# Layer boundaries: the residual's scale and shift on VectorE inside the next layer, parameter columns issued later, the second router's weights read earlier

## The chip, the cores and the metric

One core of a Trainium2 chip runs the whole program in one launch. The metric is the device time of one execution in microseconds (us). Of the kernel before there are three timed runs and one execution that was profiled.

## What is computed

The reference runs two blocks of two layers each on a sequence of 512 rows of 1024 values in float32. Each layer is a mixer, a residual sum with a layer norm, a feed-forward part, and again a residual sum with a layer norm. The mixers are RWKV, gated delta net (gdn), a state space mixer (ssd) and dilated attention; the feed-forward part is a gated linear unit (ffn) in the first block and a mixture of 32 experts with a router (MoE) in the second. The norm that stands at each of the eight boundaries is this:

```python
def _layer_norm(x, g, b):
    mu = jnp.mean(xf, -1, keepdims=True)
    var = jnp.mean(jnp.square(xf - mu), -1, keepdims=True)
    return ((xf - mu) * lax.rsqrt(var + LN_EPS) * g + b).astype(x.dtype)
...
x = _layer_norm(DEEPNORM_ALPHA * x + (1 + ga1) * y, ln_g[i, 0], ln_b[i, 0])
u = x * (1 + sc2) + sh2
```

The next layer needs the norm's output twice: at once, as the input of its matmuls, and much later, as the residual x of its own sum.

## The kernel before

The residual lies in four tiles `res[:, t]` of 128 rows by 1024 values. A layer's matmuls run with the input transposed. A float32 product is made of three matmuls of halves: `split` writes the high half of an operand with ScalarE (`uh`, `wh`, line L370) and the low half with VectorE (`ul`, `wl`, line L371). `Stream` loads the weights by SyncE (SP) into three buffers `raw` and splits them into a ring of five `wh`/`wl` slots (the pool `wsp`), some tiles ahead of TensorE.

A layer ends with `ln_tail` (L488). For each tile t it makes the last sum, the norm's statistics, and then `Norm.norm`: the mean and variance, `rs` with a power on POOL (L376), `mr` on VectorE (L2391), and the normalisation in place on ScalarE (L2396, or L2394). `Norm.trans` transposes the tile on TensorE and applies the norm's g and b, folded with the layer's own scale and shift, per partition (L615), so that the matmuls do not need `res` with g and b in it. The first matmul blocks of the next layer, the "heads" (L406), are issued here in two halves of 256 columns; the second half waits for the last tile. Then `Norm.finish` puts g and b on the residual itself, four multiplications and four additions of 128x1024 on POOL, with rows that SP loaded:

```python
with self.n.tc.issue_after(self.last):
    for t in range(NT):
        G.tensor_mul(res[:, t], res[:, t], self.g)
        G.tensor_add(res[:, t], res[:, t], self.b)
```

This runs at five boundaries, l = 0 to 3 (into the first ffn, gdn, the second ffn, ssd) and l = 5 (into attention); the last norm, l = 7, has a form of its own. Ahead of a MoE (l = 4 and 6, `keep=True`) the MoE applies it itself. A scheduler sets the order of each engine's instructions when the program is built, and it does not change at run time; each engine works through its own list in order.

Each mixer also reads small parameters and brings them into columns: for gdn the convolution's weights and the norm's gains (`gconv`, `gng`), the casts `negb` and `idb`; for ssd `sconv`, `snw`, `hv` and `dsk` (L1423, element by element, L1424 halves it). `moe_open` (L1898) reads the router's weights `rw`, `rb` and `gs` through ScalarE's DMA queue (L1914 to L1917); at the first router its calls stand well ahead of the norm, at the second right behind attention.

## Time and profile before

| what | value |
|---|---|
| median of 3 runs | 3842.15 us (3834.15 to 3850.82) |
| the profiled execution | 3842.46 us |
| its span in the trace | 3840.6 us |
| mean granted TensorE clock | 0.957 |
| TensorE busy | 3561.0 us, 93% |
| VectorE (DVE) busy | 1904.9 us, 50% |
| ScalarE (ACT) busy | 1153.1 us, 30% |
| POOL busy | 554.3 us, 14% |

The span is what the trace holds of the profiled execution; 1.9 us lie around it. In time order the stages are RWKV up to about 630 us, the first ffn (from 660), gdn (1040), the second ffn (1560), ssd (1936), the first MoE (2355), attention (2885) and the second MoE (3254).. The granted clock is 1.00 at 2.4 GHz and 0.50 at 1.2 GHz.

### The profile page before, as it was taken

To read this page: it belongs to the slowest core of one execution; us is meant where nothing else is said; L and a number is where in the kernel's file an instruction comes from. 1 tells how busy PE (TensorE), PEld (TensorE's weight loads), DVE (VectorE), ACT (ScalarE), POOL (GpSimd) and SP (SyncE) were. 2 spreads that over 40 slices of the span, in tenths; PEclk is the share of its full clock that TensorE was granted. 3 is DMA by queue.
4 is the path that set the end of the run, shared out by engine and by line. 5 is a ranking of instruction groups with operands and counts; after the bars stand their busy time and mean duration, and the time that the engine had idled before them with its cause. 6 is when DMAs were issued, how large, how long until landed. Compare 5 with 4: busy or idle time off the path is not lost. (4 is left out here: it accounts for less than half of the span.)

```text
span 3840.6 us, 53459 instructions
## 1 busy us (share of the span) xinstructions
PE 3561.0 (93%) x21818; PEld 2441.1 (64%) x21818; DVE 1904.9 (50%) x3405; ACT 1153.1 (30%) x2216; POOL 554.3 (14%) x326
## 2 busy tenths in 40 slices
PE   7999998999989998999979998999997998899998
PEld 5666656788766655788868777454446776545444
DVE  6766657433676555534469875222225344322223
ACT  4544433322343333422244432111113333211111
POOL 0111114301321120312121110200003111200001
PEclk9999998999999988999989998999998998899999
DMA  6323444223221111232323453999992224598997
GB/s 234 122 83 121 136 154 140 99 88 109 76 67 50 45 36 65 88 99 88 96 82 114 144 182 118 392 419 375 419 381 80 63 64 151 222 413 345 371 419 300
DMA packets 273357, 676.90 MB, mean 176 GB/s; under 512 B 27565, under 2 KB 166662, under 8 KB 224982
## 3 DMA queue, kind: packets, MB, share of 16 engines
q1 hardware_dynamic: 264998, 669.35, 47.1%
q10 hardware_dynamic: 7824, 3.06, 0.3%
q8 instruction: 173, 2.83, 0.3%
q0 software_dynamic: 288, 1.05, 0.1%
q14 instruction: 74, 0.61, 0.0%
HBM read 660.92 MB, written 12.48 MB: 175 GB/s over the span
## 5 line engine op out<-in xcount | busy, mean ns | idle before, releaser
L371 DVE TENSOR_TENSOR wl<-raw,wh 128x1024 fp32r<-128x1024 f32 x305 | 412.1, 1352 | 430.2 <-ACT wh L370 424.3
L384 PE MATMUL acc<-uh,wh 128*128 128x512 f32 x1384 | 559.1, 406 | 2.5 <-ACT uh L370 2.5
L370 ACT ACTIVATE wh<-raw 128x1024 fp32r<-128x1024 f32 x305 | 320.3, 1052 | 795.4 <-PE acc L384 383.5
L384 PE MATMUL acc<-uh,wl 128*128 128x512 f32 x1384 | 542.0, 392 | 0.0
L384 PE MATMUL acc<-ul,wh 128*128 128x512 f32 x1384 | 541.8, 392 | 0.0
L2046 PE MATMUL acc<-raw,xg 128*64 128x512 f32 x2048 | 448.6, 593 | 3.8 <-DMA raw<-in_moe_w_up_dram 3.8
L2046 PEld LDWEIGHTS acc<-raw,xg 128*64 128x64 f32 x2048 | 149.8, 137 | 293.3 <-issue 273.9
L384 PEld LDWEIGHTS acc<-uh,wh 128*128 128x128 f32 x1384 | 261.3, 189 | 65.5 <-issue 11.3
L384 PEld LDWEIGHTS acc<-ul,wh 128*128 128x128 f32 x1384 | 261.3, 189 | 57.2 <-issue 6.4
L384 PEld LDWEIGHTS acc<-uh,wl 128*128 128x128 f32 x1384 | 260.8, 188 | 56.3 <-issue 0.8
L257 POOL TENSOR_TENSOR raw<-raw,gar 128x1024 f32<-128x1024 f32 x60 | 155.4, 2608 | 588.5 <-DMA raw<-in_ffn_w_out_dram 341.8
L2046 PE MATMUL acc<-raw,hT 128*64 128x512 f32 x1024 | 233.7, 601 | 3.5 <-issue 1.9
L2167 DVE TENSOR_TENSOR h<-h,acc 128x512 f32<-128x512 f32 x32 | 22.0, 688 | 395.8 <-PE acc L2046 395.8
L376 POOL TENSOR_TENSOR rs<-rs,mhalf 128x1 f32<-128x1 f32 x32 | 18.9, 591 | 1184.9 <-DVE rs L375 728.6
L2046 PEld LDWEIGHTS acc<-raw,hT 128*64 128x64 f32 x1024 | 72.0, 138 | 140.5 <-issue 136.2
L2158 DVE SCALAR_TENSOR_TENSOR mrow<-acc,sg,mrow 128x512 fp32r<-128x512 f32 x64 | 47.9, 750 | 199.9 <-ACT mrow L2157 196.7
L434 PE MATMUL o<-wh,hl 128*128 128x512 f32 x352 | 138.6, 394 | 0.0
L434 PE MATMUL o<-wh,hh 128*128 128x512 f32 x352 | 138.3, 393 | 0.0
L434 PE MATMUL o<-wl,hh 128*128 128x512 f32 x352 | 136.7, 388 | 0.0
L384 PE MATMUL tp<-uh,wh 128*128 128x512 f32 x312 | 136.4, 437 | 0.0
L2046 PE MATMUL tp<-mrow,ul 128*128 128x256 f32 x512 | 130.6, 294 | 4.0 <-DVE mrow L2051 4.0
L384 PE MATMUL tp<-ul,wh 128*128 128x512 f32 x312 | 132.7, 425 | 0.0
(661 smaller groups left out, 6351.6 us busy)
## 6 DMA issues: line engine op xcount, KB each, us to landing
raw<-in_moe_w_up_dram SPq DMA_DIRECT2D x128, 1024.0 KB
raw<-in_moe_w_gate_dram SPq DMA_DIRECT2D x126, 1024.0 KB
raw<-in_moe_w_down_dram SPq DMA_DIRECT2D x74, 1024.0 KB
raw<-in_moe_w_down_dram SPq DMA_DIRECT2D x108, 512.0 KB
raw<-in_ada_w_dram SPq DMA_DIRECT2D x48, 1024.0 KB
raw<-in_ffn_w_in_dram SPq DMA_DIRECT2D x44, 1024.0 KB
raw<-in_ffn_w_out_dram SPq DMA_DIRECT2D x20, 1024.0 KB
raw<-in_attn_w_qkv_dram SPq DMA_DIRECT2D x36, 512.0 KB
```

The lines of the kernel that those rows point to most:

```text
L257: n.nc.gpsimd.tensor_mul(src, src, row[:, None, :].to_broadcast(list(src.shape)))
L370: self.nc.scalar.activation(dst_h, src, AF.Copy)
L371: self.nc.vector.tensor_sub(dst_l, src, dst_h.bitcast(F32))
L376: self.pow_ins = self.nc.gpsimd.tensor_tensor(out, out, self.mhalf[:, :out.shape[1]], op=ALU.pow).ins
L384: self.nc.tensor.matmul(ps, lhsT=l[:, k], rhs=r[:, k], start=n == 0, stop=n == 3 * NK - 1)
L434: self.nc.tensor.matmul(ps, lhsT=l[:, kx0 + k, ts], rhs=r[:, k], start=start and n == 0, stop=stop and n == 5)
L2046: self.tc.keep_in_program_order(PE.matmul(*a, **k))
L2158: V.scalar_tensor_tensor(yl[:, cs], y[half], g, yh[:, cs].bitcast(F32), op0=ALU.mult, op1=ALU.subtract)
L2167: V.tensor_tensor(to(h), to(h), of(pu), op=ALU.mult)
```

## The change

Four things change.

- At l = 0, 1, 2 and 5 the g and b of the residual are no longer applied by POOL in `finish`. The new `affine` does it on VectorE inside the next layer: in an ffn behind the third block of the first group, in gdn and in attention behind the first projection group. The row of g is loaded by SP behind the newest weight load, the row of b by POOL's queue. In an ffn the two rows have a pool of their own, in gdn and attention they take slots of the ring `wl`. At l = 3 (into ssd) POOL does it as before.
- In gdn and ssd the parameter columns, casts and exponentials are issued behind the last head matmul, split and activation (`after`).
- In ssd the two element-wise DMAs of `dsk` go from SP's queue to POOL's, and the halving of `dsk` comes later (L1482).
- The second router's weights and gains are read in `moe_small`, ahead of attention, into a pool of their own.

The diff:

```diff
@@ -347,7 +347,7 @@
-    def load_rows(self, name, parts, pool=None, q=None, rt=None):
+    def load_rows(self, name, parts, pool=None, q=None, rt=None, late=False):
@@ -361,14 +361,24 @@
         ps = self.tp(name=name + "_p")
-        nc.tensor.transpose(ps[:, :n], rt[:n, :], self.ident[:n, :n])
         out = (pool or self.const).tile([P, n], F32, name=name)
-        nc.vector.tensor_copy(out, ps[:, :n])
+        with self.after(late):
+            nc.tensor.transpose(ps[:, :n], rt[:n, :], self.ident[:n, :n])
+            nc.vector.tensor_copy(out, ps[:, :n])
         yield out
+    @contextmanager
+    def after(self, late=True):
+        with ExitStack() as es:
+            if late:
+                for i in (self.last_mm, self.last_split, self.last_act):
+                    es.enter_context(self.tc.issue_after(i))
+            yield
...
         self.nc.scalar.activation(dst_h, src, AF.Copy)
-        self.nc.vector.tensor_sub(dst_l, src, dst_h.bitcast(F32))
+        self.last_split = self.nc.vector.tensor_sub(dst_l, src, dst_h.bitcast(F32)).ins
@@ -403,8 +413,9 @@
             for l, r in ((w[0], self.uh), (w[0], self.ul), (w[1], self.uh)):
-                self.nc.tensor.matmul(ps[:, cs], lhsT=l[:, k], rhs=r[:, k, cs], start=n == 0, stop=n == 3 * NK - 1)
+                mm = self.nc.tensor.matmul(ps[:, cs], lhsT=l[:, k], rhs=r[:, k, cs], start=n == 0, stop=n == 3 * NK - 1)
                 n += 1
+        return mm.ins
@@ -506,7 +517,7 @@
         for ps, w in heads:
-            self.mm_t_half(ps, w, 1)
+            self.last_mm = self.mm_t_half(ps, w, 1)
         self.pre = [h[0] for h in heads]
@@ -574,6 +585,20 @@
+    def affine(self, tile):
+        nc, V = self.nc, self.nc.vector
+        for n, (q, f) in enumerate(((nc.sync, V.tensor_mul), (nc.gpsimd, V.tensor_add))):
+            row = tile()
+            if n:
+                q.dma_start(row, bcast_rows(self.late[n]))
+            else:
+                with self.tc.issue_after(self.st.loads[max(self.st.loads)]):
+                    q.dma_start(row, bcast_rows(self.late[n]))
+            for t in range(NT):
+                f(self.res[:, t], self.res[:, t], row)
@@ -637,7 +662,7 @@
             ln = Norm(self, pool, l)
-            hp, ep = pool("ffh"), pool("ffe", 2)
+            hp, ep, ap = pool("ffh"), pool("ffe", 2), pool("ffa", 2)
             self.load_gate(i, 1)
@@ -650,6 +675,8 @@
                     self.split(hh[:, b], hl[:, b], sg)
+                    if g is FF_GROUPS[0] and b == 2:
+                        self.affine(lambda: ap.tile([P, D], F32, name="row"))
                 last = g is FF_GROUPS[-1]
@@ -1144,16 +1171,17 @@
             negb = cn.tile([P, C], BF, name="negb")
-            V.tensor_copy(negb, self.hcv("gneg"))
             idb = cn.tile([P, P], BF, name="idb")
-            V.tensor_copy(idb, self.ident)
-            cw = self.rows_to_cols("gconv", [I["gdn_conv"][0]], pool=cn).rearrange("p (i b) -> p i b", i=4)
-            ng = self.rows_to_cols("gng", [I["gdn_norm_g"][0]], pool=cn)
-            V.tensor_scalar(ng, ng, 0.5, None, op0=ALU.mult)
             dtb = cn.tile([P, 2, H], F32, name="dtb")
...
             nc.sync.dma_start(dtb[:, 1], bcast_rows(I["gdn_a_log"][0]))
-            A.activation(dtb[:, 1], dtb[:, 1], AF.Exp)
+            cw = self.rows_to_cols("gconv", [I["gdn_conv"][0]], pool=cn, late=True).rearrange("p (i b) -> p i b", i=4)
+            ng = self.rows_to_cols("gng", [I["gdn_norm_g"][0]], pool=cn, late=True)
+            with self.after():
+                V.tensor_copy(negb, self.hcv("gneg"))
+                V.tensor_copy(idb, self.ident)
+                V.tensor_scalar(ng, ng, 0.5, None, op0=ALU.mult)
+                A.activation(dtb[:, 1], dtb[:, 1], AF.Exp)
             Q = cn.tile([P, 8, 2, C], F32, name="gQ")
@@ -1374,6 +1402,7 @@
             drain(proj(0))
+            self.affine(lambda: self.wsp.tile([P, D], F32, name="row", tag="wl"))
             for p in range(4):
@@ -1415,18 +1444,18 @@
             self.load_hc(cn, "ssd0", "attn0")
-            cw = self.rows_to_cols("sconv", [I["ssd_conv_w_2"][0], I["ssd_conv_b_2"][0]], pool=cn)
-            nw = self.rows_to_cols("snw", [I["ssd_norm_w_2"][0]], pool=cn)
+            hv = cn.tile([NH, 2], F32, name="hv")
+            nc.sync.dma_start(hv[:, 0:1], I["ssd_dt_bias_2"][0].rearrange("(h o) -> h o", o=1))
+            nc.sync.dma_start(hv[:, 1:2], I["ssd_a_log_2"][0].rearrange("(h o) -> h o", o=1))
+            cw = self.rows_to_cols("sconv", [I["ssd_conv_w_2"][0], I["ssd_conv_b_2"][0]], pool=cn, late=True)
+            nw = self.rows_to_cols("snw", [I["ssd_norm_w_2"][0]], pool=cn, late=True)
             dsk = cn.tile([P, 16], F32, name="dsk")
...
             for h in range(2):
-                nc.sync.dma_start(dsk[HS[h]], bass.AP(tensor=dv.tensor, offset=dv.offset + h, ap=[[0, 64], [2, 16]]))
-            V.tensor_scalar(dsk, dsk, 0.5, None, op0=ALU.mult)
-            hv = cn.tile([NH, 2], F32, name="hv")
-            nc.sync.dma_start(hv[:, 0:1], I["ssd_dt_bias_2"][0].rearrange("(h o) -> h o", o=1))
-            nc.sync.dma_start(hv[:, 1:2], I["ssd_a_log_2"][0].rearrange("(h o) -> h o", o=1))
-            A.activation(hv[:, 1:2], hv[:, 1:2], AF.Exp)
-            V.tensor_scalar(hv[:, 1:2], hv[:, 1:2], -1.0, None, op0=ALU.mult)
+                nc.gpsimd.dma_start(dsk[HS[h]], bass.AP(tensor=dv.tensor, offset=dv.offset + h, ap=[[0, 64], [2, 16]]))
+            with self.after():
+                A.activation(hv[:, 1:2], hv[:, 1:2], AF.Exp)
+                V.tensor_scalar(hv[:, 1:2], hv[:, 1:2], -1.0, None, op0=ALU.mult)
@@ -1449,7 +1478,8 @@
             V.tensor_scalar(ndt, ndt, 0.5, None, op0=ALU.mult)
-            V.tensor_scalar(ndec, ndec, 0.25, None, op0=ALU.mult)
+            with self.tc.issue_after(V.tensor_scalar(ndec, ndec, 0.25, None, op0=ALU.mult).ins):
+                V.tensor_scalar(dsk, dsk, 0.5, None, op0=ALU.mult)
             pe = self.tp([P, NC * NH])
@@ -1846,6 +1876,7 @@
             drain(proj(0))
+            self.affine(lambda: self.wsp.tile([P, D], F32, name="row", tag="wl"))
             with self.phase() as p2, self.tc.issue_after(self.last_act):
@@ -1906,10 +1937,16 @@
             nc.vector.tensor_copy(self.mtri, self.hcv("mtri"))
-        self.rw = self.mc.tile([P, NK, 36], F32, name="rw")
-        self.rb = self.mc.tile([P, 36], F32, name="rb")
-        self.gs = self.mc.tile([P, 2, NK], F32, name="gs")
+        if not i:
+            self.moe_small(self.mc, i, l)
+    def moe_small(self, c, i, l):
+        nc, I = self.nc, self.ins
+        self.rw = c.tile([P, NK, 36], F32, name="rw")
+        self.rb = c.tile([P, 36], F32, name="rb")
+        self.gs = c.tile([P, 2, NK], F32, name="gs")
         for j in range(2):
@@ -2373,9 +2410,12 @@
         if not keep:
-            self.g, self.b = (p.tile([P, D], F32, name="ln" + q) for q in "gb")
-            net.nc.sync.dma_start(self.g, bcast_rows(g))
-            net.nc.sync.dma_start(self.b, bcast_rows(b))
+            self.late = l in (0, 1, 2, 5)
+            self.rows = g, b
+            if not self.late:
+                self.g, self.b = (p.tile([P, D], F32, name="ln" + q) for q in "gb")
+                net.nc.sync.dma_start(self.g, bcast_rows(g))
+                net.nc.sync.dma_start(self.b, bcast_rows(b))
@@ -2425,7 +2465,10 @@
         if not self.keep:
+            self.n.late = self.rows
+        if not self.keep and not self.late:
             G, res = self.n.nc.gpsimd, self.n.res
@@ -2526,8 +2569,9 @@
         n.moe(0, 4, (P, P))
-    n.attn()
     with n.phase() as pool:
+        n.moe_small(pool("mo_w"), 1, 6)
+        n.attn()
         n.moe_open(pool, 1, 6)
```

On VectorE in gdn, behind the first projection group, before (qkv are the convolution's tiles, L1111 to L1119):

```order
L371 TENSOR_TENSOR wl<-raw,wh 128x1024
L1111 TENSOR_SCALAR qkv_9145<-xin,gconv 128x512
L1116 SCALAR_TENSOR_TENSOR qkv_9145<-xin,gconv,qkv_9145 128x511
L1116 SCALAR_TENSOR_TENSOR qkv_9145<-xin,gconv,qkv_9145 128x510
L1116 SCALAR_TENSOR_TENSOR qkv_9145<-xin,gconv,qkv_9145 128x509
L1119 SCALAR_TENSOR_TENSOR qkv_9145<-th,qkv_9145 128x512
L371 TENSOR_TENSOR wl<-raw,wh 128x1024
L1111 TENSOR_SCALAR qkv_9186<-xin,gconv 128x512
L1116 SCALAR_TENSOR_TENSOR qkv_9186<-xin,gconv,qkv_9186 128x511
```

and now:

```order
L1143 SCALAR_TENSOR_TENSOR qkv_9137<-xin,gconv,qkv_9137 128x511
L1143 SCALAR_TENSOR_TENSOR qkv_9137<-xin,gconv,qkv_9137 128x510
L600 TENSOR_TENSOR res<-res,row 128x1024
L1143 SCALAR_TENSOR_TENSOR qkv_9137<-xin,gconv,qkv_9137 128x509
L600 TENSOR_TENSOR res<-res,row 128x1024
L1146 SCALAR_TENSOR_TENSOR qkv_9137<-th,qkv_9137 128x512
L1138 TENSOR_SCALAR qkv_9178<-xin,gconv 128x512
L600 TENSOR_TENSOR res<-res,row 128x1024
L1143 SCALAR_TENSOR_TENSOR qkv_9178<-xin,gconv,qkv_9178 128x511
L600 TENSOR_TENSOR res<-res,row 128x1024
L1143 SCALAR_TENSOR_TENSOR qkv_9178<-xin,gconv,qkv_9178 128x510
L600 TENSOR_TENSOR res<-res,row 128x1024
```

The eight operations of `affine` (L600) stand between the convolution's, and the next `wl` comes behind all of them.

On VectorE into ssd, from the norm of the last tile, before:

```order
L2391 SCALAR_TENSOR_TENSOR mr<-mv,rs 128x1
L371 TENSOR_TENSOR ul<-uT_13138,uh 128x4x128
L1424 TENSOR_SCALAR dsk<-dsk 128x16
L615 TENSOR_SCALAR uT_13138<-tT,lng,lnb 128x128
L371 TENSOR_TENSOR ul<-uT_13138,uh 128x4x128
L615 TENSOR_SCALAR uT_13138<-tT,lng,lnb 128x128
L366 COPY sconv<-sconv_p 128x120
L1429 TENSOR_SCALAR hv<-hv 32x1
L371 TENSOR_TENSOR ul<-uT_13138,uh 128x4x128
L615 TENSOR_SCALAR uT_13138<-tT,lng,lnb 128x128
L366 COPY snw<-snw_p 128x16
L371 TENSOR_TENSOR wl<-raw,wh 128x1024
```

and now:

```order
L2431 SCALAR_TENSOR_TENSOR mr<-mv,rs 128x1
L381 TENSOR_TENSOR ul<-uT_13130,uh 128x4x128
L640 TENSOR_SCALAR uT_13130<-tT,lng,lnb 128x128
L381 TENSOR_TENSOR ul<-uT_13130,uh 128x4x128
L640 TENSOR_SCALAR uT_13130<-tT,lng,lnb 128x128
L381 TENSOR_TENSOR wl<-raw,wh 128x1024
L381 TENSOR_TENSOR ul<-uT_13130,uh 128x4x128
L640 TENSOR_SCALAR uT_13130<-tT,lng,lnb 128x128
L381 TENSOR_TENSOR wl<-raw,wh 128x1024
L381 TENSOR_TENSOR ul<-uT_13130,uh 128x4x128 x2
L1458 TENSOR_SCALAR hv<-hv 32x1
L1463 TENSOR_SCALAR dtrows<-acc,hv 32x512
```

`dsk` no longer stands between the last tile's `ul`, and the copies of `sconv` and `snw` and the sign of `hv` come behind them.

On POOL in the second ffn and into ssd, now:

```order
L386 TENSOR_TENSOR rs<-rs,mhalf 128x1 x3
L1455 DMA dsk<-in_ssd_d_dram 64x16x1 x2
L386 TENSOR_TENSOR rs<-rs,mhalf 128x1
L2476 TENSOR_TENSOR res<-res,lng 128x1024 x2
L2477 TENSOR_TENSOR res<-res,lnb 128x1024 x2
L2476 TENSOR_TENSOR res<-res,lng 128x1024 x2
L2477 TENSOR_TENSOR res<-res,lnb 128x1024 x2
L1535 TENSOR_TENSOR xd<-xr,dtnat 128x512 x3
```

In the list before, SP held the two DMAs of `dsk`, and POOL had the four `rs` in a row and then the same eight operations of the norm; now the DMAs stand ahead of the last tile's `rs`.

On TensorE at the second router, before:

```order
L434 MATMUL o_24677<-wl,uh 128x512
L434 MATMUL o_24677<-wh,uh 128x512
L434 MATMUL o_24677<-wh,ul 128x512
L434 MATMUL o_24677<-wl,uh 128x512
L2409 MATMUL tp<-rw,lnb 128x36 x8
L2416 MATMUL tT<-hc_ident,res 128x128 x8
L2422 MATMUL logits<-rw,uT_24626 128x36 x4
L434 MATMUL o_24678<-wh,uh 128x512
L434 MATMUL o_24678<-wh,ul 128x512
```

and now:

```order
L1797 MATMUL tp<-hc_ident,pr 128x128 x4
L1812 MATMUL po<-prT,v_24182 64x128
L1844 MATMUL tp<-cst,hc_rot 128x16 x4
L2449 MATMUL tp<-rw,lnb 128x36 x5
L1812 MATMUL po<-prT,v_24182 64x128 x7
L2449 MATMUL tp<-rw,lnb 128x36 x3
L1865 MATMUL acc<-hc_ident,cw 64x128 x16
L445 MATMUL o_24639<-wh,uh 128x512
L445 MATMUL o_24639<-wh,ul 128x512
L445 MATMUL o_24639<-wl,uh 128x512
```

The matmuls of `rw` with the norm's shift (L2409, now L2449) stand in attention's last block, ahead of the output projection.

## Rows read from the trace of the kernel before

**Rows 1.** Waits of TensorE, 655 to 690 us (line, waited for: total us, times, longest)

```profile
PE acc L406 <- DVE ul L371: 7.3, 3, 4.8
PE tT L608 <- ACT res L2396: 1.9, 1, 1.9
```

**Rows 2.** Groups by line, 655 to 690 us (xcount, busy us, mean ns)

```profile
L371 DVE TENSOR_TENSOR ul<-uT,uh 128x512 fp32r<-128x512 f32 x6 | 12.6, 2113 | 1.1 <-ACT uh L370 1.1
L2433 POOL TENSOR_TENSOR res<-res,lng 128x1024 f32<-128x1024 f32 x4 | 11.8, 2975 | 0.0
```

**Rows 3.** Three stretches: busy us of each engine, granted clock, DMA share, GB/s

```profile
655.00:690.00 35.00, 25.21 (x142) 22.14 (x141) 26.75 (x27) 19.77 (x34) 23.98 (x10) 0.85 0.27 90
1090.00:1200.00 110.00, 104.52 (x801) 73.23 (x801) 72.47 (x134) 40.64 (x99) 10.85 (x9) 1.00 0.19 58
3290.00:3400.00 110.00, 104.69 (x546) 52.18 (x548) 32.59 (x81) 15.06 (x28) 19.36 (x9) 0.96 0.85 338
```

**Rows 4.** Groups on VectorE, 1934 to 1985 us

```profile
L371 DVE TENSOR_TENSOR ul<-uT,uh 128x512 fp32r<-128x512 f32 x6 | 4.1, 686 | 1.5 <-ACT uh L370 1.5
```

**Rows 5.** Tile mr, 655 to 665 us (duration ns min/median/max)

```profile
L2391 DVE SCALAR_TENSOR_TENSOR mr<-mv,rs x2: 159/1239/2319, 656.3 to 661.3; 128x1 f32<-128x1 f32 x2
```

**Rows 6.** Timeline of VectorE, 693 to 709 us (start us, us, instruction, idle before)

```profile
693.24 1.23 DVE L371 TENSOR_TENSOR wl<-raw,wh 128x1024 fp32r<-128x1024 f32 x1 [2.96 <-ACT wh L370]
697.66 0.69 DVE L651 TENSOR_TENSOR sg<-acc,sg 128x512 f32<-128x512 f32 x1 [3.19 <-PE acc L384]
...
708.31 0.69 DVE L651 TENSOR_TENSOR sg<-acc,sg 128x512 f32<-128x512 f32 x1 [3.42 <-PE acc L384]
```

**Rows 7.** Waits of TensorE, 1036 to 1080 us

```profile
PE acc L406 <- DVE ul L371: 9.1, 4, 5.2
...
PE gng_p L364 <- DVE gconv L366: 3.1, 1, 3.1
```

**Rows 8.** Line L2197, DMAs that POOL issues (duration of the issue, and landing)

```profile
L2197 POOL DMA_DIRECT2D gar<-in_ln_b_dram x2: 622/710/797, 2438.9 to 3347.4; - x2
...
DMA to landing us min/median/max: 8.2/8.8/9.5
```

**Rows 9.** Waits of TensorE, 1555 to 1585 us

```profile
PE acc L406 <- DVE ul L371: 6.9, 3, 4.4
```

**Rows 10.** Waits of TensorE, 1934 to 1985 us

```profile
PE sconv_p L364 <- ACT uT L612: 14.0, 1, 14.0
PE acc L406 <- ACT uh L370: 2.3, 2, 2.1
PE acc L406 <- DVE ul L371: 2.1, 2, 1.7
```

**Rows 11.** Waits of VectorE, 1934 to 1985 us

```profile
DVE dsk L1424 <- DMA dsk<-in_ssd_d_dram: 16.0, 1, 16.0
```

**Rows 12.** Tile dsk, 1900 to 2000 us, its issue by SyncE

```profile
L1423 SPq DMA_DIRECT2D dsk<-in_ssd_d_dram x2: 708/1983/3258, 1932.8 to 1933.5; - x2
```

**Rows 13.** Waits of TensorE, 2878 to 2932 us

```profile
PE acc L406 <- ACT uh L370: 6.2, 1, 6.2
PE acc L406 <- DVE ul L371: 6.0, 2, 3.6
PE tT L608 <- ACT res L2394: 5.6, 2, 3.8
```

**Rows 14.** Waits of TensorE, 3235 to 3290 us

```profile
PE tp L2409 <- DMA rw<-moe_w_router_expert_dram: 12.3, 1, 12.3
```

**Rows 15.** Tile rw at the second router, 3225 to 3262 us

```profile
L2409 PE MATMUL tp<-rw,lnb x16: 400/407/407, 3254.2 to 3257.4; 128*128 128x36 f32 x16
...
L1916 ACTq DMA_DIRECT2D rw<-moe_w_router_expert_dram x1: 446/446/446, 3234.0 to 3234.0; - x1
```

**Rows 16.** Tile rw at the first router, 2280 to 2360 us

```profile
L2409 PE MATMUL tp<-rw,lnb x16: 194/279/279, 2351.1 to 2352.7; 128*128 128x36 f32 x16
...
L1916 ACTq DMA_DIRECT2D rw<-moe_w_router_expert_dram x1: 460/460/460, 2285.8 to 2285.8; - x1
```

## The prediction

> **What bounds the kernel.** The page comes first. TensorE is busy for 93% of the span, VectorE for 50%, ScalarE for 30%, POOL for 14%. With such a share of TensorE, a change pays where TensorE stands still or runs at the lower clock, so the second view is its waits by stretch, around each boundary between two layers. Read at the first boundary [rows 1]: in 35 us it stands 7.3 us for VectorE's `ul` and 1.9 us for ScalarE's `res`. The third view, the groups by line, says why VectorE is late [rows 2]: a `ul` takes 2113 ns in the mean, though the same split takes 686 ns at the ssd boundary [rows 4], and while these run POOL works at the residual in pieces of 2975 ns. The plainest sign is `mr`, an operation on 128x1: 159 ns for one tile, 2319 ns for the next [rows 5]. So POOL's 128x1024 operations hold up VectorE's small ones, and these stand in the chain norm, transpose, split, matmul that ends the boundary. The fourth view, the table of stretches, gives the clock: granted 0.85 in the mean over these 35 us [rows 3], that is, part of them at 1.2 GHz; behind the boundaries it is 1.00 and 0.96.
>
> **First ffn (l = 0).** Removed from the boundary: the eight operations of POOL. TensorE's waits are 7.3 + 1.9 = 9.2 us. The clock lost 0.15 x 35 = 5.3 us, of which 25.21/35 fell on busy time [rows 3], 3.8 us. The most to be had is thus 13 us. VectorE agrees: six `ul` lose 6 x (2113 - 686) = 8.6 us and `mr` 2.2 us, 10.8 in all. The serial chain of the last tile stays, so I take 9.5, with 4.8 (the longest wait alone) and 13 as ends. Added: eight two-input operations of 128x1024 on VectorE. The nearest row is an undisturbed `wl` of the same shape, 1.23 us [rows 6], so 8 x 1.23 = 9.8 us. They stand between splits. One block of TensorE takes 708.31 - 697.66 = 10.65 us [rows 6] and uses two `wl`; with five slots VectorE may run about 27 us ahead. I cost the operations at nothing; without that cover they would cost 9.8 us.
>
> **gdn (l = 1).** TensorE's waits for `ul` and for the column copy are 9.1 + 3.1 = 12.2 us [rows 7]. The copies and casts leave the chain as POOL does. I take 10, with 5.2 and 17 as ends (12.2, and as much clock as above with a little more). Here the affine is less well covered: between 1090 and 1200 us VectorE is busy 72.47 of 110 us, and TensorE 104.52 [rows 3], so both are near their limits, its eight operations stand ahead of the next `wl`, and its two rows hold two of five slots. Of its 9.8 us I take half, 5 us, as lost. The ends are 0 and 19: all of it, and one wait for a row of 9.5 us, the longest landing of a DMA of POOL's [rows 8]. Net gain 5.
>
> **Second ffn (l = 2).** The pattern of the first: the `ul` waits are 6.9 us [rows 9]. I take 9, ends 4.4 and 13.
>
> **ssd (l = 3).** TensorE stands 14.0 us for the column transpose `sconv_p`, because `uT` is late [rows 10], and that is late because VectorE stands 16.0 us for `dsk` at the head of its list [rows 11]. All of the 14.0 goes when `dsk` is moved. But POOL's affine remains here, and worked in that time while VectorE stood idle; now it meets the `ul` of the last tile. That is the first ffn's boundary over again, 9.2 us, of which 2.3 + 2.1 = 4.4 us are paid already [rows 10]. So 14.0 - 4.8 = 9.2. The two DMAs of `dsk` move to POOL ahead of the last `rs`. What POOL needs to issue them no row shows. For SP it was 0.71 + 3.26 = 3.97 us [rows 12]; POOL issued a row to 128 partitions in 0.62 to 0.80 us [rows 8]. If its time went with the pieces, 1024 elements against 128 rows, it would be 8 x 0.71 = 5.7 us each and 11.4 in all. I take 1.2 us as lost (POOL idles ahead of that `rs`), with 0 and 11.4 as ends. Net 8, ends -2 and 14.
>
> **Attention (l = 5).** The waits are 6.2 + 6.0 + 5.6 = 17.8 us [rows 13]. Part of the 5.6 for `res` is the chain itself, so I take 13, ends 6.2 and 19. The affine lies under a projection phase with TensorE as the bound; its rows take two slots for a while: 2 us, ends 0 and 10. Net 11.
>
> **Second router.** TensorE stands 12.3 us for the expert weights [rows 14]; their DMA was issued at 3234.0 and the first matmul began at 3254.2 [rows 15], so it landed 20 us after its issue. At the first router the issue was at 2285.8 and the matmul at 2351.1 [rows 16], 65 us, with no such wait. Reading ahead of attention makes it so here. I take 12, ends 6 and 16 (the second router then waits for its own norm, or gets clock back as well). Moved along: six small DMAs that ScalarE issues, 446 ns for such a one [rows 15], now ahead of attention, 6 x 0.45 = 2.7 us, of which I take 1.
>
> **The sum.** 9.5 + 5 + 9 + 8 + 11 + 12 - 1 = 53.5 us. The profiled execution took 3842.46 us, 0.3 above the median of the runs, so 3842.5 - 53.5 = 3789 us, 1.4% less.
>
> **Rivals.** (a) *Half is given back*, 15%. The serial chain per tile, not VectorE's slowness, is the limit: TensorE's waits change names from `ul` to `res` or `uT`, and the clock stays low in the gaps. For it: 5.6 us for `res` in attention are such waits. Against: the `ul` waits are as long as the excess of VectorE. Half of 53.5 gone gives 3816 us.
>
> (b) *dsk costs POOL its proportional price*, 8%. The last `rs` into ssd is then 11.4 us late, less the overlap, and 8 turns into about -2: 3799 us.
>
> (c) *The rows are late and VectorE stands*, 6%, slower. The multiplications wait for the row of g at the head of VectorE's list, with the splits and the layer's own work behind them, and then the additions for b. With both rows asked for at once and landing in 9 us, the cover of 27 us in an ffn, and of 3 slots or 16 us in gdn and attention, is about enough. If they come one after the other and each takes 20 us, as the router's did [rows 15], VectorE is held 2 x 20 + 9.8 = 50 us, and TensorE stands 50 - 27 = 23 in each ffn and 50 - 16 = 34 in gdn and attention, 114 in all: 3789 + 114 - 7 already counted = 3896 us. The sign turns where a row takes about 13 us (8 x 13 + 4 x 9.8 - 2 x 27 - 2 x 16 = 57). Against: outside the MoE the loads use a fifth to a quarter of the DMA time [rows 3].
>
> (d) *The MoE swallows its 12*, 6%. It is bound by its weight loads (DMA share 0.85, 338 GB/s [rows 3]), so an earlier start would not pass through if the loads were already ahead of it. Then 3801 us. Against: its buffers are full when the norm begins, so the loads wait for the matmuls.
>
> (e) *POOL's own DMAs are held up by VectorE*, 5%. POOL and VectorE hold each other up, as `mr` shows, by 2319 - 159 = 2.2 us at a time [rows 5]. If each of the six DMAs that move to POOL (four rows of b, two of `dsk`) were late by this and nothing hid it, that would be 13 us: 3802 us. Against: the DMAs of POOL landed in 8.2 to 9.5 us [rows 8] with VectorE half busy. The Trainium skill, SBUF — State Buffer, "SBUF: two separate sides", states such a rule against this change: GpSimd writes the descriptors of the DMAs that it issues, and cannot while VectorE copies in its two-port mode. No row of before shows this.
>
> **Chances.** 60% for the forecast, then 15, 8, 6, 6 and 5. About 0.5%, 19 us, is what a measurement of this kernel can tell from no change: faster means below 3823 us, slower above 3862. The forecast, (b), (d), (e) and two thirds of (a) are faster, 89%; a third of (a) and a little of (c) the same, 6%; the rest slower, 5%. The forecast's own range is 3768 to 3812, from the ends above with not all of them at once; (a) reaches 3822. I give 3762 to 3820.
>
> **What will show it.** No POOL operation of the norm at l = 0, 1, 2, 5; `ul` near 0.69 us there, but near 2.1 into ssd; the TensorE waits for `ul` at 3 us or less at each of the four; no wait for `dsk` or `rw`; VectorE's affine at 1.2 us each, without a wait for `row`. A wait of `res` for the DMA of `row`, a late last `rs` into ssd, or more TensorE waits between 1090 and 1300 us would show the steps on the added work wrong. A time above 3823 would make the prediction wrong as a whole.

## The result and the profile after

The changed kernel takes 3801.39 us (median of 4 runs, 3792.99 to 3806.93), the kernel before 3846.2 us (4 runs): a ratio of 0.9879, 95% interval 0.9858 to 0.9899. That is 1.2% faster; 1.4% was forecast. The profiled execution took 3798.41 us, 44 less than that of before. The page's first line now reads:

```profile
PE 3556.3 (94%) x21818; PEld 2428.2 (64%) x21818; DVE 1900.4 (50%) x3437; ACT 1151.8 (30%) x2216; POOL 470.4 (12%) x300
```

VectorE is as busy as before, with 32 operations more, since it no longer loses time to POOL. To see where the 44 us come from, the span is cut at instructions that both timelines hold: the last `mr` of each norm, and the end of the last head matmul. A "boundary" runs from the one to the other, a layer from there to the next norm's last `mr`.

| stage | before us | after us | gain | forecast |
|---|---|---|---|---|
| RWKV and what precedes it (unchanged) | 661.3 | 656.5 | 4.8 | 0 |
| boundary into the first ffn | 25.8 | 14.3 | 11.5 | 9.5 |
| first ffn | 353.9 | 353.9 | 0 | 0 |
| boundary into gdn | 26.0 | 14.3 | 11.7 | 10 |
| gdn | 489.9 | 511.1 | -21.2 | -5 |
| boundary into the second ffn | 25.2 | 14.2 | 11.0 | 9 |
| second ffn | 353.9 | 354.0 | -0.1 | 0 |
| boundary into ssd | 34.7 | 28.1 | 6.6 | 8 |
| ssd | 400.8 | 398.5 | 2.3 | 0 |
| first MoE | 526.7 | 533.2 | -6.5 | 0 |
| boundary into attention | 31.7 | 14.0 | 17.7 | 13 |
| attention, to the second router's norm | 348.0 | 338.9 | 9.1 | 12 - 2 - 1 |
| second MoE | 562.7 | 565.6 | -2.9 | 0 |

The four boundaries without POOL's affine are all at 14 us. TensorE's waits at the first of them, where it stood 9.2 us [rows 1], and VectorE's groups there [rows 2], are now:

```profile
PE acc L416 <- ACT uh L380: 1.7, 2, 1.5
PE acc L416 <- DVE ul L381: 0.2, 1, 0.2
```

```profile
L600 DVE TENSOR_TENSOR res<-res,row 128x1024 f32<-128x1024 f32 x8 | 9.3, 1217 | 1.6 <-DMA row<-in_ln_g_dram 1.6
L381 DVE TENSOR_TENSOR wl<-raw,wh 128x1024 fp32r<-128x1024 f32 x7 | 8.6, 1222 | 6.3 <-ACT wh L380 6.3
L381 DVE TENSOR_TENSOR ul<-uT,uh 128x512 fp32r<-128x512 f32 x6 | 4.1, 688 | 2.4 <-ACT uh L380 2.4
```

At these boundaries the granted clock came back as well. The first one and the one into attention, all instructions (busy us of PE, PEld, DVE, ACT and POOL, clock, DMA share, GB/s), before:

```profile
661.30:687.10 25.80, 16.48 (x98) 15.34 (x98) 19.91 (x12) 11.72 (x22) 22.80 (x8) 0.80 0.22 74
2898.10:2929.90 31.80, 19.46 (x105) 18.64 (x105) 25.66 (x18) 11.37 (x24) 21.61 (x8) 0.66 0.11 34
```

and now:

```profile
656.50:670.70 14.20, 12.62 (x98) 11.96 (x98) 8.13 (x12) 11.62 (x22) 0.74 (x1) 1.00 0.41 129
2878.10:2892.10 14.00, 12.68 (x101) 12.27 (x101) 9.17 (x17) 10.54 (x23) 0.00 (x0) 0.97 0.23 70
```

Length less busy time of TensorE is the time that it stands. At the first boundary it fell by 7.7 us and the busy time, at the higher clock, by 3.9; into attention by 11.0 and 6.8.

A `ul` takes 688 ns where it took 2113, the wait for it fell from 7.3 to 0.2 us, and the affine costs 8 x 1.2 us on VectorE with a wait of 1.6 us for its row, all of it under the splits' lead: the ffn behind it is as long as before.

Into ssd, where POOL's affine stays, the wait for `dsk` is gone, and the collision has taken its place, as forecast. TensorE's waits [rows 10], and POOL's timeline around the DMAs of `dsk`:

```profile
PE acc L416 <- DVE ul L381: 9.4, 3, 7.3
PE acc L416 <- ACT uh L380: 4.2, 2, 4.0
```

```profile
1915.47 1.75 POOL L1455 DMA_DIRECT2D dsk<-in_ssd_d_dram  x2 [2.25 <-PE tT L633]
1917.65 0.56 POOL L386 TENSOR_TENSOR rs<-rs,mhalf 128x1 f32<-128x1 f32 x1 [0.42 <-DVE rs L385]
```

POOL issued both DMAs in 1.75 us and then waited for VectorE, not VectorE for it. At the second router the matmuls of `rw` run at 3195 us, ahead of attention's output projection, and wait for nothing [rows 14, 15]:

```profile
L2449 PE MATMUL tp<-rw,lnb x16: 279/279/299, 3195.5 to 3198.3; 128*128 128x36 f32 x16
```

Two stages went the other way, gdn and the first MoE. The first experiments are about gdn.

### The profile page after: what moved, and what is told of

It is laid out like the page before. It is cut to its first block, busy times and chain, and to the rows that moved or that the text cites. A ratio compares the mean times of both kernels' runs of the same rounds, so it can differ in the third digit from the quotient of the medians.

```text
span 3796.6 us, 53463 instructions
## 1 busy us (share of the span) xinstructions
PE 3556.3 (94%) x21818; PEld 2428.2 (64%) x21818; DVE 1900.4 (50%) x3437; ACT 1151.8 (30%) x2216; POOL 470.4 (12%) x300
## 5 line engine op out<-in xcount | busy, mean ns | idle before, releaser
L394 PE MATMUL acc<-uh,wh 128*128 128x512 f32 x1384 | 558.7, 406 | 2.5 <-ACT uh L380 2.5
L394 PE MATMUL acc<-ul,wh 128*128 128x512 f32 x1384 | 541.3, 391 | 0.0
L394 PE MATMUL acc<-uh,wl 128*128 128x512 f32 x1384 | 540.9, 391 | 0.0
L394 PEld LDWEIGHTS acc<-uh,wh 128*128 128x128 f32 x1384 | 260.8, 189 | 65.5 <-issue 11.3
L394 PEld LDWEIGHTS acc<-ul,wh 128*128 128x128 f32 x1384 | 260.9, 188 | 56.9 <-issue 6.4
L394 PEld LDWEIGHTS acc<-uh,wl 128*128 128x128 f32 x1384 | 260.5, 188 | 56.1 <-issue 0.8
L394 PE MATMUL tp<-uh,wh 128*128 128x512 f32 x312 | 139.3, 446 | 0.0
L394 PE MATMUL tp<-uh,wl 128*128 128x512 f32 x312 | 134.9, 432 | 0.0
L394 PE MATMUL tp<-ul,wh 128*128 128x512 f32 x312 | 134.6, 431 | 0.0
```

The lines of the kernel that those rows point to most:

```text
L394: self.nc.tensor.matmul(ps, lhsT=l[:, k], rhs=r[:, k], start=n == 0, stop=n == 3 * NK - 1)
```

## The experiments

The times below are medians of each run's own executions; ratios are to the kernel before on the same chip. Stage times are from each run's profile.

| run | median us | ratio, 95% interval | gdn us | other stage us |
|---|---|---|---|---|
| changed | 3801.4 | 0.9879, 0.9858 to 0.9899 | 511.1 | |
| gdn_none | 3785.2 | 0.9841, 0.9816 to 0.9867 | 485.4 | |
| gdn_pool | 3792.5 | 0.9862, 0.9836 to 0.9889 | 487.3 | boundary into gdn 27.7 |
| gdn_p2 | 3777.8 | 0.9821, 0.9790 to 0.9852 | 479.4 | |
| gdn_cols | 3798.3 | 0.9881, 0.9853 to 0.9910 | 495.4 | boundary into gdn 13.9 |
| router_late | 3786.6 | 0.9852, 0.9819 to 0.9885 | 509.8 | first MoE 528.9 |
| ssd_late | 3791.8 | 0.9854, 0.9808 to 0.9899 | 503.0 | boundary into ssd 16.1, ssd 413.1 |
| pool_next | 3810.9 | 0.9899, 0.9871 to 0.9928 | 505.8 | attention 352.2 |
| dsk_sp | 3794.8 | 0.9857, 0.9825 to 0.9889 | 497.0 | boundary into ssd 28.1 |
| ssd_cols | 3803.1 | 0.9889, 0.9856 to 0.9918 | 492.7 | boundary into ssd 30.1 |
| combined | 3771.6 | 0.9801, 0.9770 to 0.9832 | 477.6 | boundary into ssd 16.5, ssd 411.1 |
| combined_g3 | 3770.8 | 0.9806, 0.9781 to 0.9831 | 477.5 | boundary into ssd 16.5, ssd 413.4 |
| combined_ssdpool | 3767.9 | 0.9799, 0.9772 to 0.9827 | 488.6 | boundary into ssd 27.0, ssd 400.6 |

**gdn_none: no affine in gdn.**

```diff
             drain(proj(0))
-            self.affine(lambda: self.wsp.tile([P, D], F32, name="row", tag="wl"))
             for p in range(4):
```

> From the changed kernel, the affine of gdn is left out (the residual of that layer lacks g and b); nothing else is changed. In the two profiles the boundary into gdn gained 11.7 us, but the gdn layer behind it, from the end of the heads to the last mr of the next norm, went from 489.9 to 511.1 us. Theory A: the affine inside gdn (8 operations on VectorE, two slots of wl, two row loads) costs these 21 us. Then the layer is at 490 here and the kernel at about 3780 us. Theory B: the moved columns, or a lower granted clock that has nothing to do with the affine, cost them. Then the layer stays at 511 and the kernel at 3801 us.

The layer is at 485.4 us and the kernel at 3785: theory A, though some 5 us short of its gain in total.

**gdn_pool: POOL again at l = 1.**

```diff
-            self.late = l in (0, 1, 2, 5)
+            self.late = l in (0, 2, 5)
```

(and no call of `affine` in gdn)

> From the changed kernel, l = 1 alone goes back to POOL in finish. Both theories expect the boundary into gdn to lose most of its 11.7 us again (26 us from the last mr to the end of the heads, where it is 14.3). Theory A (the affine inside gdn costs 21 us): the layer is at 490, and the kernel at 3801 + 11 - 21 = 3791 us, faster than with the move. Theory B: the layer stays at 511, and the kernel is at 3812 us.

The boundary is at 27.7 us, the layer at 487.3, the kernel at 3792.5: near theory A. Boundary and layer together are at 515.0 us here and at 525.4 in the changed kernel's profile, where the move lost more inside the layer than it gained. The layer varies from execution to execution, though: with the mean of the five profiles below (502.7) the changed form is at 517.0, about even, and the two intervals of the whole kernel overlap.

**gdn_p2: the same work later in gdn.**

```diff
             drain(proj(0))
-            self.affine(lambda: self.wsp.tile([P, D], F32, name="row", tag="wl"))
             for p in range(4):
+                if p == 2:
+                    self.affine(lambda: self.wsp.tile([P, D], F32, name="row", tag="wl"))
```

> From the changed kernel, the affine of gdn is issued ahead of the third pair of heads (p = 2) and not behind the first projection group. Theory A, place: it costs because it delays the first chain; here the layer is at 490 to 497 us and the kernel at 3780 to 3787. Theory A, amount: 9.8 us of VectorE and two slots cost the same anywhere in this layer: 511 and 3801 us. Theory B: 511 and 3801 us as well.

479.4 us and 3777.8 us, below even what the theory of place expected: it is the place. The same eight operations and two slots cost nothing that these runs can tell ahead of the third pair of heads. The intervals of this kernel and of the changed one do not meet.

How the place costs is seen in the tables of stretches. First the changed kernel, in steps of 30 us from 30 us behind the heads' end (1038.9 us), all instructions:

```profile
1069.00:1099.00 30.00, 26.95 (x134) 22.11 (x133) 27.98 (x40) 11.68 (x30) 5.63 (x5) 1.00 0.20 63
1099.00:1129.00 30.00, 27.43 (x265) 21.64 (x263) 27.37 (x48) 14.11 (x38) 5.51 (x4) 1.00 0.24 73
1129.00:1159.00 30.00, 25.19 (x264) 15.93 (x261) 13.23 (x30) 7.88 (x20) 0.00 (x0) 0.76 0.11 34
```

The same three stretches, the projection's matmuls alone (line L394; the columns are PE, PEld, clock, DMA share, GB/s):

```profile
1069.00:1099.00 30.00, 24.65 (x106) 19.19 (x104) 1.00 0.20 63
1099.00:1129.00 30.00, 17.38 (x67) 12.28 (x67) 1.00 0.24 73
1129.00:1159.00 30.00, 8.01 (x18) 3.84 (x18) 0.76 0.11 34
```

And those of gdn_p2, the same line, as far behind its heads' end (1045.4 us):

```profile
1075.00:1105.00 30.00, 22.06 (x91) 16.24 (x89) 1.00 0.24 71
1105.00:1135.00 30.00, 16.88 (x62) 11.17 (x62) 1.00 0.12 36
1135.00:1165.00 30.00, 18.45 (x54) 8.80 (x54) 1.00 0.11 36
```

With the affine early VectorE is busy 28 and 27 of 30 us, the convolutions and the chain of the first heads come later, and TensorE meanwhile takes projection matmuls ahead (106 in place of 91). These were the filling beside the chain's small products. In the third stretch 18 of them are left where gdn_p2 has 54, TensorE works mostly at small products, and the granted clock, 1.00 until then, is 0.76 in the mean. In gdn_p2 it stays at 1.00.

The clock does not follow each time. The third stretch of ssd_cols, a later run with the same gdn, line L394 as above:

```profile
1142.00:1172.00 30.00, 9.25 (x28) 4.40 (x28) 1.00 0.11 36
```

28 projection matmuls are left, the clock is 1.00, and TensorE is busy for 25.2 of the 30 us, as in the changed kernel. In all six profiles with VectorE's affine early in gdn the filling is spent by this stretch (17 to 28 matmuls, against 52 to 54 in the eight others); the clock falls there to 0.74 to 0.77 in four of them, and in none of the others. A part of the difference between 18 and 28 is the lower clock itself. So the spent filling is shown, and the clock goes with it in four of six; no run separates the one from the other.

Over the whole layer, changed, gdn_none and gdn_p2 in turn:

```profile
1038.90:1550.00 511.10, 458.88 (x3274) 320.64 (x3272) 302.43 (x575) 185.58 (x511) 74.48 (x58) 0.89 0.15 49
```

```profile
1052.40:1537.80 485.40, 435.67 (x3275) 306.76 (x3273) 295.20 (x568) 186.06 (x511) 73.60 (x57) 0.94 0.15 49
```

```profile
1045.40:1524.80 479.40, 427.72 (x3274) 300.73 (x3272) 302.43 (x575) 186.19 (x511) 76.38 (x58) 0.95 0.16 52
```

TensorE stands 52.2, 49.7 and 51.7 us. In these three nearly all of the difference is busy time at a lower clock. It is not the same in each execution: four later runs have gdn in the changed kernel's form, and their profiles show 509.8, 503.0, 497.0 and 492.7 us. The mean of the five is 502.7. In the form of gdn_p2 there are four profiles, 479.4, 477.6, 477.5 and 488.6, mean 480.8. The least costly of the first kind, from ssd_cols:

```profile
1052.20:1544.90 492.70, 436.08 (x3274) 308.04 (x3273) 304.90 (x576) 185.41 (x511) 74.02 (x59) 0.94 0.16 51
```

It has the clock of gdn_none, and 56.6 us of standing. TensorE stands 52.2 to 56.7 us in the five (mean 55.2) and 50.2 to 51.7 in the four (50.7); it is busy for 447.5 us in the mean of the five and 430.1 in that of the four, with the same matmuls. So of the mean difference of 22 us the early place costs 4.5 us by waits and 17 by the clock, which ranges from 0.89 to 0.94 in the five and from 0.93 to 0.96 in the four. The slowest of the four, combined_ssdpool, has a fall of the clock of its own, at a later place in the layer. Against the two profiles without this work in gdn, gdn_none and gdn_pool (mean 486.4), the early place costs 16 us.

**gdn_cols: the columns of gdn early again.**

```diff
-            cw = self.rows_to_cols("gconv", ..., pool=cn, late=True)...
-            ng = self.rows_to_cols("gng", ..., pool=cn, late=True)
-            with self.after():
+            cw = self.rows_to_cols("gconv", ..., pool=cn)...
+            ng = self.rows_to_cols("gng", ..., pool=cn)
+            if True:
```

> From the changed kernel, the columns, casts and the exponential of gdn are issued early again, as before; the affine stays inside gdn. Theory A: the boundary into gdn takes 1 to 4 us more than 14.3, the layer stays at 511, and the kernel is at 3802 to 3805 us. Theory B in the form that the columns cost it: the layer is back at 490 and the kernel at 3782 to 3785 us.

The boundary is at 13.9 us, not the 15 to 18 that were expected without the move, the layer at 495.4, within the range of the five, the kernel at 3798. Once POOL is out of the way the moved columns of gdn are worth nothing that this can tell.

**router_late: the router's loads in attention.**

```diff
-        n.moe_small(pool("mo_w"), 1, 6)
+        n.mow = pool("mo_w")
         n.attn()
...
             for p in range(4):
+                if p == 1:
+                    with self.tc.issue_after(self.last_act):
+                        self.moe_small(self.mow, 1, 6)
```

> From the changed kernel, the second router's six small loads are issued behind the second projection group of attention, where the changed kernel has them in the last 65 us of the first MoE. In the two profiles the first MoE went from 526.7 to 533.2 us (from its norm's last mr to the next norm's). Theory C: the some 2900 small packets of these loads hold up the MoE's last weight loads and cost these 6.5 us. Then the MoE is at 527 here, the router still waits for nothing, and the kernel is at 3795 us. Theory D: the 6.5 us have another cause (the next norm's own chain, the clock); the MoE stays at 533 and the kernel at 3801.

In the changed kernel, ScalarE issues these loads at 2815 us, when the MoE still streams weights. Of its profile, the queue that carries them, from 2805 to 2850 us (packets, MB, share), and a wait of TensorE between 2800 and 2880 us:

```profile
q10 hardware_dynamic: 2912, 0.17, 4.4%
```

```profile
PE acc L2083 <- DMA raw<-in_moe_w_up_dram: 2.6, 2, 1.3
```

The six loads, 0.17 MB, come in 2912 packets. With the loads in attention the wait is gone, and the MoE is at 528.9 us here and at 528.7 to 531.4 in the three combined runs, where the nine profiles with the loads as changed have 532.7 to 534.2. So theory C holds for 4 of the 6.5 us. The rest, to the 526.7 of before, lies at the stage's end: in its last 20 us TensorE stood 6.3 us before, at a clock of 0.86, and 7.4 to 7.6 us in every profile with the change, at 0.76 to 0.81. Why, is open. The total says more than it should: in the profiled execution RWKV, which is unchanged, took 647.7 us, 8.8 less than in the changed kernel's profile.

**ssd_late: VectorE's affine in ssd too.**

```diff
-            self.late = l in (0, 1, 2, 5)
+            self.late = l in (0, 1, 2, 3, 5)
...
             for g in range(4):
+                if g == 1:
+                    self.affine(lambda: self.wsp.tile([P, D], F32, name="row", tag="wl"))
```

> From the changed kernel, the norm into ssd (l = 3) loses its affine on POOL too, and gets it on VectorE ahead of the second group of the scan. Theory E: POOL's operations beside VectorE's cost that boundary what they cost the others. Then it goes from 28.1 us to 14 or 15, the ssd layer (398.5 us) gains no more than 3 us in length, and the kernel is at 3788 to 3791 us. Rival, as in gdn: the affine inside the layer takes back what the boundary gains; the layer is at 410 and the kernel at 3799 to 3803.

The boundary falls to 16.1 us, so POOL's operations cost it 12 us as they cost the others; and the layer goes from 398.5 to 413.1. Theory E is right on the boundary and the rival on the layer, and by the stage times the exchange is about even. The kernel's 3791.8 us would speak for theory E, but its four executions go from 3777 to 3810, so the total decides nothing. In the changed kernel VectorE is busy for 91 and 88 of 100 us in two stretches of this layer:

```profile
1996.00:2096.00 100.00, 99.52 (x535) 81.30 (x534) 91.06 (x164) 39.26 (x59) 10.16 (x7) 1.00 0.41 126
2096.00:2196.00 100.00, 97.18 (x525) 79.15 (x523) 87.73 (x170) 44.46 (x68) 13.12 (x10) 1.00 0.41 133
```

and in ssd_late the sooner end of the heads uncovers another load:

```profile
PE snw_p L366 <- DMA snw_r<-in_ssd_norm_w_dram: 4.7, 1, 4.7
```

SP issues this load when the heads end, in both kernels; its transpose ran 2.4 us later in the changed kernel, without a wait, and 7.1 us later here. The wait is 4.7 of the 10 to 15 us that the layer loses (398.5 to 403.6 us in the profiles with POOL's affine there), and it comes ahead of VectorE's added work.

**pool_next: the new places, but POOL's operations.**

```diff
-        for n, (q, f) in enumerate(((nc.sync, V.tensor_mul), (nc.gpsimd, V.tensor_add))):
+        for n, (q, f) in enumerate(((nc.sync, nc.gpsimd.tensor_mul), (nc.gpsimd, nc.gpsimd.tensor_add))):
```

> From the changed kernel, the affine stays at its new places inside the next layers but runs on POOL and not on VectorE. Theory F: what the boundaries gained comes from the time at which the affine runs, not from the engine. Then the four boundaries stay at 14.0 to 14.3 us, the two ffn stay at 353.9 under their cover, and only gdn and attention change, by the 2.1 us that each operation of POOL may hold up one of VectorE's: 8 x 2.1 = 17 in place of 9.8, so gdn at 511 to 519 and the kernel at 3801 to 3815. Rival: the engine matters everywhere, since VectorE is slowed at the new places as it was at the old; each ffn gets longer by 5 to 10 us as well and the kernel is at 3820 or more.

Theory F: the four boundaries are at 14.0 to 14.6 us, both ffn at 353.9, and the kernel is at 3811. What the boundaries gained comes from when the affine runs, not from the engine. The engine shows in one long wait of TensorE each in gdn and attention:

```profile
PE acc L1279 <- DVE nn L1275: 36.2, 12, 16.2
```

```profile
PE acc L1760 <- DVE wmask L1882: 17.3, 1, 17.3
```

The first is gdn's (the longest such wait of the changed kernel was 3.7 us), the second attention's (5.3 us in the changed kernel, 1.9 before), where the copy of the mask stands behind `wl` splits: VectorE waited 15.5 and 10.2 us there for slots that the rows held until POOL was done. Attention takes 352.2 us for 338.9. In gdn the forecast of 511 to 519 us did not come: 505.8 us lies within the five profiles of VectorE's affine at the same place, with other waits and a clock of 0.93.

**dsk_sp: dsk's DMAs by SyncE again.**

```diff
-                nc.gpsimd.dma_start(dsk[HS[h]], ...)
+                nc.sync.dma_start(dsk[HS[h]], ...)
```

> From the changed kernel, the two element-wise DMAs of dsk go back to SyncE's queue; their halving stays behind the boundary. Theory G: it was the halving at the head of VectorE's list that cost the boundary into ssd, not the queue. Then the boundary stays at 28 us (27.4 to 28.4 in the runs so far) and the kernel at 3801. Rival: the queue counts, since SyncE issues these two in 4 us ahead of weight loads that the heads need. Then the boundary is at 31 to 33 us and the kernel at 3804 to 3806.

The boundary is at 28.1 us: theory G. The queue does not count; that the place of the halving does, follows with the next run, where the columns and `hv` go back and `dsk` does not.

**ssd_cols: the columns of ssd early again.**

```diff
-            cw = self.rows_to_cols("sconv", ..., pool=cn, late=True)
-            nw = self.rows_to_cols("snw", ..., pool=cn, late=True)
+            cw = self.rows_to_cols("sconv", ..., pool=cn)
+            nw = self.rows_to_cols("snw", ..., pool=cn)
...
-            with self.after():
+            if True:
                 A.activation(hv[:, 1:2], hv[:, 1:2], AF.Exp)
```

> From the changed kernel, the columns of ssd (sconv, snw) and the exponential and sign of hv are issued early again, as before; dsk stays as changed. Theory H: only dsk counted. Then the boundary into ssd stays at 28 us and the kernel at 3801. Rival: hv is next in line, since its two loads take SyncE 2.2 and 3.3 us to issue and VectorE then stands for hv instead. Then the boundary is at 32 to 38 us and the kernel at 3805 to 3811.

The boundary is at 30.1 us, between the two, and neither names the wait:

```profile
PE snw_p L366 <- DMA snw_r<-in_ssd_norm_w_dram: 13.5, 1, 13.5
```

With `dsk` away, the next load in line is that of `snw`, for which TensorE itself stands. It costs only 2 us, because POOL's affine runs on in that time: the waits for `ul` are 2.7 us here, 9.4 in the changed kernel. So the moved columns count in ssd, but little while POOL's affine stays there; and with the halving late the boundary is still 4.6 us shorter than before (34.7).

**combined, combined_g3, combined_ssdpool.** The first has the affine of gdn ahead of the third pair, that of attention behind the second projection group (`if p == 1:`), the router's loads as in router_late and ssd as in ssd_late.

> All that the runs so far point to in one kernel: the affine of gdn ahead of the third pair of heads, that of attention behind its second projection group, that of ssd on VectorE ahead of the second group, and the router's loads behind attention's second projection group. If theories A (place), C and E hold and add up: 3778 (gdn ahead of the third pair, measured) - 6 - 11 - 3 = 3758 us. If C and E are wrong: 3775 to 3778 us.

3771.6 us: 14 above the sum, of which 11 are the exchange in ssd, which gave nothing, and 2 the router's gain, 4 and not 6. Attention is at 335.7 to 336.3 us in the three combined profiles: with the affine behind its second group the 3 us for the mask come back. The other two change ssd alone.

```diff
-                if g == 1:
+                if g == 3:
                     self.affine(lambda: self.wsp.tile([P, D], F32, name="row", tag="wl"))
```

> From the combined kernel, the affine of ssd stands ahead of the fourth group of the scan, not ahead of the second. In ssd_late the boundary gained 12 us and the layer lost 12. Theory place, as in gdn: late in the layer the affine costs nothing; the ssd layer goes from 411 to 400 us and the kernel from 3771 to 3760. Theory amount: the layer stays at 411 and the kernel at 3771.

```diff
-            self.late = l in (0, 1, 2, 3, 5)
+            self.late = l in (0, 1, 2, 5)
...
-                if g == 1:
-                    self.affine(lambda: self.wsp.tile([P, D], F32, name="row", tag="wl"))
```

> From the combined kernel, the affine into ssd goes back to POOL in finish, as before and as changed. If the exchange in ssd is even, as the stage times say (16.5 + 411.1 against 28.1 + 398.5 to 402), the kernel stays at 3770 to 3773 us. If the move was a gain that the other stages hid, 3778 or more; if it was a loss, 3765 or less.

The ssd layer is 413.4 us with the affine late and 400.6 without: a later place does not help in ssd. That it is the amount is not shown by this, for the wait for `snw` is in both forms (3.7 us here and in combined), and TensorE's busy time is 390 to 391 us where it was 383 to 385, at a clock of 0.97 in place of 0.98 to 0.99. Ahead of the fourth group VectorE has room (67.7 of 100 us busy between 2196 and 2296 us in the changed kernel); why the layer is no shorter there is open. All three kernels are about 2% faster than before and can be told apart neither from each other nor, by their totals, from gdn_p2.

## Why the prediction was right, and where it was off

The direction, the size (53.5 forecast, 44 and 45 measured) and the range (3762 to 3820) held. The total is closer than its terms, which is luck in part: in the two profiles the four boundaries gave 10 us more than forecast and gdn 16 less, the two MoE lost 9, and RWKV, which is unchanged, gave 4.8 by a higher clock. The terms:

- **The boundaries into ffn, gdn, ffn and attention** were right in mechanism and too small: 9.5, 10, 9 and 13 forecast, 11.5, 11.7, 11.0 and 17.7 measured. Into the first ffn I had kept back 3.5 of 13 us for the serial chain of the last tile; it needs about 2 us of waiting, as the 1.7 for `uh` shows, and the clock gave back the 3.8 us that I had put for it (3.9). Into attention I had put nothing for the clock, and it gave 6.8. `ul` near 0.69 us and the waits below 3 us were forecast and came. The Trainium skill, SBUF — State Buffer, "Who interferes with whom", says that a VectorE instruction with two inputs in SBUF and a GpSimd instruction that reads SBUF shut each other out for the whole instruction; 2113 ns against 688 for the same `ul` agrees with it.
- **The ffn's affine at nothing** was right: 353.9 us in both, with 1.6 us of waiting for a row, where I had forecast none.
- **gdn's affine at 5 us**, with ends of 0 and 19, is the step that failed: 21 us in the two profiles, and 16 in the mean of five against the two without it. I looked at what its operations would hold up on VectorE, and that part was about right: 4.5 us of waits. I did not ask what TensorE would do while VectorE was late. It used up the projections that were to run beside the chain, and the lower clock cost 17 us more in the mean, against the later place. That the fall of the clock comes from the spent filling is what the stretches suggest; two of six executions spent it without that fall, so the link is not shown.
- **ssd at 8** was right in its two halves: the wait for `dsk` went, the collision with POOL came (9.4 + 4.2 us of waits), 6.6 us net at the boundary. The 2.3 in the layer are no part of it: nine other profiles with POOL's affine there have 400.3 to 403.6 us, 400.8 before. The 1.2 us for POOL's issue of `dsk` were 1.75 of POOL's time, and 0 for the chain.
- **The second router at 12, less 1 for ScalarE**: the wait of 12.3 us went, but I costed the moved DMAs by their issue alone and not by where their data would fall. They fell into the one stage that is bound by its loads, and 4 of the MoE's 6.5 us are theirs. Attention paid 3.4 us more for its mask, behind VectorE's wait for the row of g:

```profile
DVE res L600 <- DMA row<-in_ln_g_dram: 5.7, 1, 5.7
```

Of the rivals, (a) did not come: the waits fell away, did not change names, and the clock rose to 0.97 and more. (b) did not: 1.75 us, not 11.4. (c) is seen in its mildest form, three waits for a row of g of 9.0 us in all, 5.7 of them in attention. (d) did not: the second MoE grew by 2.9 us, not by 12 (0.9 to 6.5 in the thirteen profiles; the cause is open). (e) did not: in no stage of the changed kernel did an instruction wait for a row of b, which POOL's queue brings. The rule of the Trainium skill that stood beside it, SBUF — State Buffer, "SBUF: two separate sides", is neither confirmed nor refuted: only in pool_next does anything wait for a row of b, 6.3 us in two waits, and there POOL, which does the arithmetic too, issued these two DMAs only after its own multiplications.

## What to carry to other kernels

Work that is wanted only later should not run beside the chain that ends a stage, on an engine that slows the chain's own, as POOL did VectorE here; where it goes instead is decided stage by stage, by measuring. In a stage where dense matmuls fill the gaps of a latency chain, as in gdn, added work on another engine at its start can make TensorE use up the filling early, so try it later in the stage, and read the granted clock as well as the waits; in ssd a later place did not help. A small load that is moved forward may cost little at its issue and more where its packets land, 4 us in the MoE here: look at the DMA share of that stretch first.

## What was not expected of the hardware

The first stage, up to the first norm, is the same in all these kernels, and TensorE stands 58 to 60 us in it in both runs below. Yet it took 647.7 us in router_late and 669.9 in gdn_none:

```profile
0.00:647.70 647.70, 589.68 (x5984) 397.96 (x5985) 426.32 (x912) 280.61 (x595) 103.37 (x74) 0.97 0.42 143
```

```profile
0.00:669.90 669.90, 609.52 (x5983) 411.02 (x5984) 428.19 (x911) 280.82 (x595) 103.65 (x73) 0.92 0.40 138
```

20 of the 22 us are busy time at the granted clock, 0.97 against 0.92, with the same instructions. That is 22 us of spread between executions from one stage, half of what the whole change is worth; a stage's own time in the profile tells more of a change than the total of one run.
